# Attention scores on alternating halves of the array, masks added by VectorE, and one projection less in each mixer

## The chip, the cores and the metric

One NeuronCore of a Trainium2 chip runs the whole program. The metric is the device time of one execution in microseconds (us), from the first to the last instruction of the core with what lies around them; lower is better. TensorE multiplies matrices, VectorE (DVE) and ScalarE (ACT) do the elementwise work, and SyncE (SP) starts the transfers.

## The reference, cut to what matters

Two blocks of two layers each on 256 tokens of width 1024. The first block's layer is a feed-forward, a mixer of three kinds of attention, a second feed-forward, and a gated per-layer input. The second block works on the same tokens and on a context of 256 tokens: its layer 0 has a convolution, its layer 1 a windowed attention with sinks over own and context keys.

```python
def masked_softmax(s, mask):
    p = jax.nn.softmax(jnp.where(mask, s.astype(jnp.float32), NEG_BIG), axis=-1)
    return jnp.where(mask, p, 0.0)
# mixer: 4 "nsa" heads (compressed, selected and window keys; one key head of 64 for all),
#        4 "diff" heads (two softmaxes over 32 features each, subtracted), 8 "fox" heads (forget gates):
s = jnp.einsum('bqhd,bkhd->bhqk', qb, k) * scale + (cq[..., :, None] - cT[..., None, :])   # fox
# second block, layer 1: 16 query heads, 4 key heads, |i - j| <= 128, a sink for each head
p = jax.nn.softmax(jnp.concatenate([s_win, s_ctx, sinks], axis=-1), axis=-1)
```

## The kernel before, in words

All is in float32. A matrix of weights comes in tiles of 128 x 1024 (512 KB), and each tile is split into a high part (ACT, a rounded fp32r copy) and a low part (DVE, the rest). A linear layer is then three fp32r products for each 128 x 128 weight block and 256 tokens (`mm3`); this is nearly all of TensorE's work. A product of plain fp32 operands (scores, transposes, values) is one instruction in the code and two MATMUL records in the trace.

**The order is planned.** Streams of work (the main stream, workers for attention heads, the context's stream, the vectors of the adaptive modulation `ada`) are generators that yield before each group of products. `plan()` runs them against `Model`, a simple clock for each engine with prices in ns, and writes down which stream goes on when; the kernel replays that list, so each engine's instructions lie in a fixed order. When no operand of the main work is there, the plan takes a group of a filler stream (context or `ada`).

**The mixer** (one in each of the first block's two layers; about 297 to 470 and 1048 to 1232 us). `project(k)` makes queries and keys with features on partitions, two weight tiles a call, nine calls a layer. `kcmp`, `vcmp`, `kslc` and `kwin` have 64 columns each; their tiles hold these columns twice (`cols_tile(W, l, c, 64, 2)`), so that both halves of the 128 partitions get a copy. `PA` and `PB` hold queries and keys of two heads in a chunk, head i of the pair on partitions 64 i to 64 i + 63. `softmax` (12 calls a layer: 4 for nsa, 4 for diff, 4 for fox) works on such a pair: for head 0 and then head 1 it takes a bank of PSUM, and for the two blocks of 128 queries (against 128 and 256 keys) it issues the score product on that head's 64 partitions (32 for diff; for fox a second product of 16 rows, `LT` and `RT`, adds the gates) and then a bf16 product of the identity with the causal mask (`identb`, `caus`) into the same bank. DVE reduces the maximum, ACT takes the exponential with its sum. `compressed` does the same for 16 compressed keys with 8 small score products, each followed by a mask product. The scaled probabilities are transposed by TensorE and multiplied with the values on 64 of the columns for each head (`values`).

**The second attention** (`attention2`, scores from 2679 us). Three workers take eight chunks c of two heads; `scores(w, c, p, P)` does head p: for each block of queries one product with the own keys (64 rows, 256 columns), one mask product, one product with the context's keys, then the maximum over 512, the sink, and the exponential. PSUM has 8 banks for all streams; the output's projection holds four of them from chunk 0 on.

All products of the scores, masks, values and linear layers are issued at L544, transposes at L561; DVE's `reduce` is L506, `tt` L479, `ts` L486; ACT's `act` is L473. Tiles `m`, `k`, `f`, `fh` are activation buffers, `w` weights, `p` banks of PSUM, `a` raw `ada` and `phi` tiles, `masksb` the masks.

## Time and profile before

| | |
|---|---|
| median of 3 runs | 3006.87 us (3004.06 to 3012.88) |
| profiled execution, span | 3003.3 us |
| TensorE busy | 2944.3 us, 98% |
| VectorE, ScalarE busy | 1957.7 us, 65%; 1409.8 us, 47% |
| mean granted TensorE clock | 0.971 |

The profiled execution is one more execution than the three that are timed; its span, from the first to the last instruction, lies 3.6 us under their median. A matmul's busy time in the profile includes its way through the array, so groups of products overlap one another; what a product costs in a full stream is read from the distance between starts. The clock is given as a share of 2.4 GHz: 0.50 is 1.2 GHz.

### The profile page before, as it was taken

The numbers are of one execution on the slowest core, as the hardware profiler recorded it, in microseconds if no ns is written. First come the engines' busy times: TensorE is split into PE (matmuls) and PEld (weight loads), VectorE is DVE, ScalarE is ACT, GpSimd is POOL, SyncE is SP. The second block draws the span as 40 slices with busy tenths as digits, with TensorE's granted clock in tenths as the row PEclk, the third lists the DMA queues.
The fourth block names the chain that finished last, engine by engine and source line by source line (L and its number), as shares of the span: only waits on it lengthen the run. The fifth ranks groups of instructions, "written<-read, shape, count | busy, mean of one in ns | idle before, by whom it ended". The sixth has DMA issues, their size and how long they took to land.

```text
span 3003.3 us, 56163 instructions
## 1 busy us (share of the span) xinstructions
PE 2944.3 (98%) x23428; PEld 2743.5 (91%) x23428; DVE 1957.7 (65%) x3312; ACT 1409.8 (47%) x2208; POOL 0.2 (0%) x4
## 2 busy tenths in 40 slices
PE   8999999999999999999899999999999999999998
PEld 8989869999999986899789999989999999976898
DVE  5457556656655665588878668888865565566554
ACT  4445334544544543354454554444554454444443
POOL 0000000000000000000000000000000000000000
PEclk9999889999999988899999999999999999999999
DMA  8766524655655554355665556565665565551453
GB/s 291 278 227 212 185 99 134 210 188 174 219 188 190 197 176 143 113 189 184 207 228 181 184 202 200 183 213 183 207 203 185 169 213 193 180 192 35 144 183 119
DMA packets 153278, 555.84 MB, mean 185 GB/s; under 512 B 16320, under 2 KB 26176, under 8 KB 152896
## 3 DMA queue, kind: packets, MB, share of 16 engines
q1 hardware_dynamic: 152304, 550.40, 54.8%
q8 instruction: 184, 3.01, 0.4%
q10 hardware_dynamic: 720, 1.85, 0.2%
q14 instruction: 70, 0.57, 0.1%
HBM read 551.14 MB, written 1.05 MB: 184 GB/s over the span
## 4 chain that ended last, share of the span: by engine, by line
PE 93%; DMA 3%; DVE 2%; ACT 1%; issue 0%; SPq 0%; ACTq 0%; DVEq 0%
PE p L544 92%; DMA a<-ada_w 2%; PE p L561 1%; DMA a<-phi_k 0%; DMA r<-W 0%; DVE m L479 0%; DVE w L479 0%; ACT m L473 0%; DMA a<-phi_v 0%; ACT f L473 0%; DVE m_qn L506 0%; DVE m L494 0%; DMA m_cE<-lam 0%; DVE m L486 0%; SPq L526 0%
## 5 line engine op out<-in xcount | busy, mean ns | idle before, releaser
L544 PE MATMUL p<-m,w 128*128 128x256 f32 x10992 | 1391.1, 284 | 8.0 <-ACT w L473 5.6
L544 PEld LDWEIGHTS p<-m,w 128*128 128x128 f32 x10992 | 1345.8, 191 | 31.9 <-issue 10.3
L479 DVE TENSOR_TENSOR w<-r,w 128x1024 fp32r<-128x1024 f32 (+1 forms) x888 | 1058.6, 1215 | 366.7 <-ACT w L473 365.2
L473 ACT ACTIVATE w<-r 128x1024 fp32r<-128x1024 f32 (+1 forms) x888 | 899.5, 1044 | 370.9 <-PE p L544 280.4
L544 PE MATMUL p<-k,w 128*128 128x256 f32 x4224 | 538.9, 282 | 0.0
L544 PEld LDWEIGHTS p<-k,w 128*128 128x128 f32 x4224 | 515.5, 188 | 9.4 <-issue 5.0
L544 PE MATMUL p<-f,w 128*128 128x256 f32 x3600 | 473.2, 287 | 0.0
L544 PEld LDWEIGHTS p<-f,w 128*128 128x128 f32 x3600 | 449.8, 192 | 9.5 <-issue 5.7
L473 ACT ACTIVATE k<-p 128x256 f32<-128x256 f32 (+1 forms) x200 | 80.7, 404 | 460.9 <-PE p L544 435.6
L479 DVE TENSOR_TENSOR k<-k,p 128x256 f32<-128x256 f32 x176 | 73.9, 420 | 252.8 <-ACT k L473 252.7
L544 PE MATMUL p<-fh,w 128*128 128x256 f32 x1776 | 234.0, 285 | 0.1
L544 PEld LDWEIGHTS p<-fh,w 128*128 128x128 f32 x1776 | 220.7, 191 | 7.5 <-issue 4.9
L479 DVE TENSOR_TENSOR k<-k,k 128x256 fp32r<-128x256 f32 (+1 forms) x176 | 74.9, 425 | 85.5 <-ACT k L473 85.5
L473 ACT ACTIVATE k<-k 128x256 fp32r<-128x256 f32 (+1 forms) x176 | 73.6, 418 | 104.1 <-DVE k L479 104.1
L544 PE MATMUL p<-a,csf 128*32 128x384 f32 x768 | 90.6, 558 | 20.8 <-DMA a<-ada_w 20.8
L494 DVE SCALAR_TENSOR_TENSOR m<-m,vec,m 128x241 f32<-128x241 f32 (+14 forms) x240 | 101.6, 471 | 0.0
L494 DVE SCALAR_TENSOR_TENSOR f<-fh,vec,f 128x241 f32<-128x241 f32 (+14 forms) x240 | 100.8, 471 | 0.0
L473 ACT ACTIVATE m<-m 128x512 f32<-128x512 f32 (+3 forms) x117 | 62.5, 553 | 75.6 <-DVE m L479 35.9
L506 DVE TENSOR_REDUCE m_qn<-p 128x1 f32<-128x128 f32 (+2 forms) x128 | 51.3, 435 | 66.6 <-PE p L544 66.5
L473 ACT ACTIVATE k<-p,m_qn 128x128 f32<-128x128 f32 x96 | 39.4, 417 | 86.2 <-DVE m_qn L506 77.8
L473 ACT ACTIVATE f_sq<-p 128x256 f32<-128x256 f32 x66 | 25.0, 379 | 108.3 <-PE p L544 108.3
L544 PE MATMUL p<-m 64*128 64x128 f32 (+1 forms) x192 | 66.2, 430 | 0.0
(221 smaller groups left out, 1511.8 us busy)
## 6 DMA issues: line engine op xcount, KB each, us to landing
r<-W SPq DMA_DIRECT2D x880, 512.0 KB, 4.3
a<-ada_w SPq DMA_DIRECT2D x96, 768.0 KB, 5.1
a<-phi_k SPq DMA_DIRECT2D x8, 512.0 KB, 6.8
a<-phi_v SPq DMA_DIRECT2D x8, 512.0 KB, 3.5
m<-xT SPq DMA_DIRECT2D x4, 256.0 KB, 4.9
r<-W SPq DMA_DIRECT2D x8, 128.0 KB, 4.7
f<-ctxT ACTq DMA_DIRECT2D x1, 1024.0 KB, 10.7
out<-m SPq DMA_DIRECT2D x4, 256.0 KB, 2.5
```

Source lines behind the costliest of these rows:

```text
L473: self.nc.scalar.activation(out, in_, func, **kw)
L479: self.nc.vector.tensor_tensor(out=out, in0=a, in1=b, op=op)
L494: self.nc.vector.scalar_tensor_tensor(out, a, s, b, op0=op0, op1=op1)
L506: self.nc.vector.tensor_reduce(out, in_, axis=AX, op=op, negate=True)
L544: self.nc.tensor.matmul(out, l, r, start=start, stop=stop, skip_group_check=True)
L561: self.nc.tensor.transpose(out, in_, ident[:k, :k])
```

## The change

- **Scores.** `softmax`, `scores` and the compressed scores take the banks of both heads first and issue one group in which the products of head 0 and head 1 alternate: one on partitions 0 to 63 (or 32 of them), the next on 64 to 127. Fox's product of the gates has 64 rows in place of 16, most of them zero. Before, all of one head's products stood ahead of the other's.
- **Masks.** The mask products on TensorE go (48 in each mixer's pairs, 8 in its compressed scores, and 32 in the second attention). In place of `reduce`, DVE runs `masked`: it adds the mask (bf16, in SBUF) to the scores, turns the sign, writes them back to PSUM and takes the minimum, in one instruction; ACT's exponential then has scale -1. The compressed scores get a `tt` with the mask and then the maximum. `scores` scales both heads' sums at once.
- **Projections.** Eight calls a layer in place of nine: `kcmp` and `vcmp` share a tile, `kslc` and `kwin` share a tile, each column once. `rope_kv` turns the last two with one product and copies them to the other half of the partitions (2 ACT copies of 64 partitions). `compressed` reads its blocks accordingly. The rotation of the nsa queries, the prefix sums and the flags of the fox heads come one `project` earlier.
- **The plan's prices.** A product of 256 fp32r columns is priced 118.2 ns (109.1 before), plain fp32 2.4 ns more, the groups of scores and values with sums of their own, and a group of scores counts 128 rows. The plan of the whole kernel is made anew with these.

```diff
-    masks = np.zeros((128, 288), np.float32)
-    masks[:, :128] = np.where(p[None, :] > p[:, None], NEG, 0.0)
-    masks[:, 128:256] = np.where(p[None, :] < p[:, None], NEG, 0.0)
-    masks[:, 256:] = np.where(okc, 0.0, NEG).reshape(128, 32)
+    masks = np.zeros((128, 672), np.float32)
+    masks[:, :128] = np.where(p[None, :] < p[:, None], NEG, 0.0)
+    masks[:, 512:640] = np.where(p[None, :] > p[:, None], NEG, 0.0)
+    masks[:, 640:] = np.where(okc, 0.0, NEG).reshape(128, 32)
...
-            return max(4 * n / 2.4, 212.0) + 2.4
-        return max(n / 2.4, 94.0 if r.dt == F32R else 53.0) + 2.4
+            return max(4 * n / 2.4, 212.0) + 4.8
+        if r.dt == F32R:
+            return max(0.4508 * n, 106.0) + 2.8
+        return max(n / 2.4, 53.0) + 2.4
...
+    def masked(self, ps, mask, ng):
+        if self.model:
+            self.model.dve(140, 1.04, [ps, ng], [ps, mask])
+        else:
+            self.nc.vector.tensor_tensor_reduce(ps, ps, mask, -1.0, 3e38, OP.add, OP.min, ng)
...
-        rows = 32 * min(g[1].t.shape[1] for g in group)
+        rows = rows or 32 * min(g[1].t.shape[1] for g in group)
         m.pe(cost or sum(m.pe_cost(l, r, r.n) for _, l, r, _, _ in group), rows, reads, writes)
...
-        PC = R.tmp((128, 2, 256), "of", 1)
-        dst = ([PA[:, i:i + 2] for i in (0, 2, 4, 6)] + [PB[:, i:i + 2] for i in (0, 2, 4, 6)] + [PC])
-        keys = [cols_tile(W, l, 256, 64, 2), cols_tile(W, l, 320, 64, 2),
+        PC = R.tmp((128, 256), "of", 1)
+        keys = [cols_tile(W, l, 256), tuple(piece(W, l, kc * 128, kc * 128 + 128, c0, c0 + 64, 0, kc * 128 + q0)
+                                            for kc in range(8) for c0, q0 in ((384, 0), (512, 64))),
                 cols_tile(W, l, 652), cols_tile(W, l, 780), cols_tile(W, l, 908), cols_tile(W, l, 1036),
-                cols_tile(W, l, 0), cols_tile(W, l, 128),
-                cols_tile(W, l, 384, 64, 2), cols_tile(W, l, 512, 64, 2)]
+                cols_tile(W, l, 0), cols_tile(W, l, 128)]
         keys += [cols_tile(W, l, 1420 + 128 * i) for i in (0, 1, 4, 5, 2, 3, 6, 7)]
-        slot = [8, 2, 3, 0, 1, 4, 6, 5, 7]
-        scale = {0: Q_SCALE, 2: D_SCALE, 4: Q_SCALE, 5: Q_SCALE}
+        dst = [None, PA[:, 4:6], PA[:, 6:8], PA[:, 0:2], PB[:, 0:2], PB[:, 4:6], PB[:, 2:4], PB[:, 6:8]]
+        scale = {1: D_SCALE, 3: Q_SCALE, 4: Q_SCALE, 6: Q_SCALE}
...
         def project(k):
             def evac(_, p):
-                d = slot[k]
-                if d in scale:
-                    self.act(dst[d], p, AF.Copy, scale=scale[d])
+                if k == 0:
+                    self.act(PC, p[:, 0])
+                    self.act(PA[:, 2], p[:, 1])
+                elif k in scale:
+                    self.act(dst[k], p, AF.Copy, scale=scale[k])
                 else:
-                    self.cp(dst[d], p)
+                    self.cp(dst[k], p)
             yield from self.lin(R, xs, keys[2 * k:2 * k + 2], evac)
+        def rope_kv():
+            cos, sin = self.rope1[:, 0], self.rope1[:, 1]
+            ps = yield from R.bank((128, 256))
+            raw = PA[:, 2]
+            yield from self.mm(ps, self.con_("perm_n"), raw, True, True)
+            t = R.tmp((128, 2, 256), "sq", 2)[:, 0]
+            self.tt(t, ps, sin, OP.mult)
+            R.banks.put(ps)
+            self.tt(raw, raw, cos, OP.mult)
+            self.tt(PA[64:128, 3], raw[64:128], t[64:128], OP.add)
+            self.tt(PA[0:64, 2], raw[0:64], t[0:64], OP.add)
+            self.act(PA[0:64, 3], PA[64:128, 3])
+            self.act(PA[64:128, 2], PA[0:64, 2])
...
-            for p in range(2):
-                pb = slice(64 * p, 64 * p + 64)
-                ps = yield from R.bank((128, 2, 2, 16))
-                for qb in range(2):
-                    for hh in range(2):
-                        yield from self.mms([(ps[:, qb, hh], PA[pb, hh, qb * 128:qb * 128 + 128], kc[pb], True, False),
-                                             (ps[:, qb, hh], identb, self.maskc[:, qb * 16:qb * 16 + 16], False, True)])
-                self.reduce(NG[:, p], ps, OP.max, negate=True)
+            pss = []
+            for _ in range(2):
+                pss.append((yield from R.bank((128, 2, 2, 16))))
+            yield from self.mms([(pss[p][:, qb, hh], PA[half(p), hh, qb * 128:qb * 128 + 128], kc[half(p)], True, True)
+                                 for qb in range(2) for hh in range(2) for p in range(2)], 1800.0)
+            mc = self.masks[:, 640:672].rearrange("p (q o c) -> p q o c", q=2, o=1).to_broadcast([128, 2, 2, 16])
+            for p, ps in enumerate(pss):
+                self.tt(E[:, p], ps, mc, OP.add)
+                R.banks.put(ps)
+                self.reduce(NG[:, p], E[:, p], OP.max, negate=True)
                 ngb = NG[:, p].rearrange("t q (h o) -> t q h o", o=1).to_broadcast([128, 2, 2, 16])
-                self.tt(E[:, p], ps, ngb, OP.add)
-                R.banks.put(ps)
+                self.tt(E[:, p], E[:, p], ngb, OP.add)
...
-        def softmax(P, sm, ng, qk):
+        def softmax(P, sm, ng, qk, cost=930.0):
+            pss = []
             for i in range(2):
-                ps = yield from R.bank((128, 384))
+                pss.append((yield from R.bank((128, 384))))
+            group = []
+            for qb in range(2):
+                ops = [qk(i, slice(qb * 128, qb * 128 + 128), 128 * (qb + 1)) for i in range(2)]
+                for k in range(len(ops[0])):
+                    group += [(pss[i][:, seg[qb]], *ops[i][k], k == 0, k == len(ops[0]) - 1) for i in range(2)]
+            yield from self.mms(group, cost, 128)
+            for i, ps in enumerate(pss):
                 for qb in range(2):
-                    n = 128 * (qb + 1)
-                    o = ps[:, seg[qb]]
-                    ops = qk(i, slice(qb * 128, qb * 128 + 128), n)
-                    yield from self.mms([(o, a, b, k == 0, False) for k, (a, b) in enumerate(ops)]
-                                        + [(o[:, n - 128:n], identb, self.caus, False, True)])
+                    self.masked(ps[:, seg[qb]], self.masks[:, 512 - 128 * qb:640], ng[:, i, qb:qb + 1])
                 for qb in range(2):
-                    self.reduce(ng[:, i, qb:qb + 1], ps[:, seg[qb]], OP.max, negate=True)
-                for qb in range(2):
-                    self.act(P[:, i, seg[qb]], ps[:, seg[qb]], AF.Exp, bias=ng[:, i, qb:qb + 1],
+                    self.act(P[:, i, seg[qb]], ps[:, seg[qb]], AF.Exp, scale=-1.0, bias=ng[:, i, qb:qb + 1],
                              accum_out=sm[:, i, qb:qb + 1])
...
-                b = slice(64 * i, 64 * i + 16)
-                k = 2 * j + i
+                b, k = half(i), 2 * j + i
                 self.ts(RT[b], cT[b], fm[b, 2 + k:3 + k], fm[b, 10 + k:11 + k], OP.mult, OP.add)
             def qk(i, q, n):
-                b = slice(64 * i, 64 * i + 16)
-                return [(PB[half(i), j, q], PB[half(i), 4 + j, :n]), (LT[b, q], RT[b, :n])]
+                b = half(i)
+                return [(PB[b, j, q], PB[b, 4 + j, :n]), (late[0][b, q], RT[b, :n])]
             P = yield from self.take(R.wk, (128, 2, 384))
-            yield from softmax(P, sm, ng, qk)
+            yield from softmax(P, sm, ng, qk, 1760.0)
...
+        self.spawn(roped(rope_kv(), fl_ + "kv"), 0)
         yield from project(3)
+        def nsa_rope():
+            yield from ropes[1]
+            yield from self.until(fl_ + "kv")
+        self.spawn(roped(nsa_rope(), fl_ + "nsa"), 0)
+        self.spawn(prefix(), 0)
         yield from project(4)
-        self.spawn(roped(ropes[1], fl_ + "nsa"), 0)
-        self.spawn(prefix(), 0)
         yield from project(5)
+        self.flags.add(fl_ + "fox0")
         yield from project(6)
-        self.flags.add(fl_ + "fox0")
         yield from project(7)
-        yield from project(8)
...
-        def scores(w, c, p, P):
+        def scores(w, c, P):
             sm, ng, es = w.small
-            h = head_of(c, p)
-            b = slice(64 * p, 64 * p + 64)
-            sk = self.vec[:, so + h:so + h + 1]
+            sk = [self.vec[:, so + head_of(c, p):so + head_of(c, p) + 1] for p in range(2)]
             for qb in range(2):
-                ps = yield from R.bank((128, 512))
-                ql = q[b, c, qb * 128:qb * 128 + 128]
-                off = 128 * (1 - qb)
-                yield from self.mms([(ps[:, 0:256], ql, k[b, c // 4], True, False),
-                                     (ps[:, off:off + 128], self.identb, (self.caus, self.anti)[qb], False, True)])
-                yield from self.mm(ps[:, 256:512], ql, self.kc2[b, c // 4], True, True)
-                n1 = ng[:, p, qb:qb + 1]
-                self.reduce(n1, ps, OP.max, negate=True)
-                self.stt(n1, sk, -1.0, n1, OP.mult, OP.min)
-                self.act(P[:, qb], ps, AF.Exp, bias=n1, accum_out=sm[:, p, qb:qb + 1])
-                self.act(es[:, p, qb:qb + 1], sk, AF.Exp, bias=n1)
-                R.banks.put(ps)
-            self.tt(sm[:, p], sm[:, p], es[:, p], OP.add)
-            self.recip(sm[:, p], sm[:, p])
-            for qb in range(2):
-                self.ts(P[:, qb], P[:, qb], sm[:, p, qb:qb + 1], None, OP.mult)
+                pss = []
+                for p in range(2):
+                    pss.append((yield from R.bank((128, 512))))
+                at = 256 * (1 - qb)
+                group = []
+                for kk, a in ((k[:, c // 4], at), (self.kc2[:, c // 4], 256 - at)):
+                    for p in range(2):
+                        b = slice(64 * p, 64 * p + 64)
+                        group.append((pss[p][:, a:a + 256], q[b, c, qb * 128:qb * 128 + 128], kk[b], True, True))
+                yield from self.mms(group, 1160.0, 128)
+                for p, ps in enumerate(pss):
+                    n1 = ng[:, p, qb:qb + 1]
+                    self.masked(ps, self.masks[:, 128 * (1 - qb):128 * (1 - qb) + 512], n1)
+                    self.stt(n1, sk[p], -1.0, n1, OP.mult, OP.min)
+                    self.act(P[:, p, qb], ps, AF.Exp, scale=-1.0, bias=n1, accum_out=sm[:, p, qb:qb + 1])
+                    self.act(es[:, p, qb:qb + 1], sk[p], AF.Exp, bias=n1)
+                    R.banks.put(ps)
+            self.tt(sm, sm, es, OP.add)
+            self.recip(sm, sm)
+            for p in range(2):
+                for qb in range(2):
+                    self.ts(P[:, p, qb], P[:, p, qb], sm[:, p, qb:qb + 1], None, OP.mult)
...
-            for p in range(2):
-                yield from scores(w, c, p, P[:, p])
+            yield from scores(w, c, P)
...
-            for kb in range(4):
-                src = (v, self.vc2)[kb // 2]
-                yield from self.mms([(O[64 * p:64 * p + 64], src[:, kb % 2, (2 * (c // 4) + p) * 64:][:, :64],
-                                      T[:, p, kb], kb == 0, kb == 3) for p in range(2)], 480.0)
+            yield from self.mms([(O[64 * p:64 * p + 64], (v, self.vc2)[kb // 2][:, kb % 2, (2 * (c // 4) + p) * 64:][:, :64],
+                                  T[:, p, kb], kb == 0, kb == 3) for kb in range(4) for p in range(2)], 2230.0)
```

## Rows read from the trace of the kernel before

**Rows 1.** The page: busy times, granted clock in 40 slices, the chain's shares by engine.

```profile
PE 2944.3 (98%) x23428; PEld 2743.5 (91%) x23428; DVE 1957.7 (65%) x3312; ACT 1409.8 (47%) x2208; POOL 0.2 (0%) x4
...
PEclk9999889999999988899999999999999999999999
...
PE 93%; DMA 3%; DVE 2%; ACT 1%; issue 0%; SPq 0%; ACTq 0%; DVEq 0%
```

**Rows 2.** Timeline of TensorE, full products: start us, us, line, out<-in, form, records.

```profile
642.38 5.84 PE L544 MATMUL p<-m,w 128*128 128x256 f32 x48
648.06 1.11 PE L544 MATMUL p<-k,w 128*128 128x256 f32 x8
```

**Rows 3.** Timeline of TensorE, one nsa pair's scores in the second mixer.

```profile
1176.11 0.48 PE L544 MATMUL p<-m 64*128 64x128 f32 x2
1176.53 0.23 PE L544 MATMUL p<-masksb,identb 128*128 128x128 bf16 x1
1176.68 0.70 PE L544 MATMUL p<-m 64*128 64x256 f32 x2
1177.31 0.23 PE L544 MATMUL p<-masksb,identb 128*128 128x128 bf16 x1
...
1178.74 0.28 PE L561 MATMUL p<-con,f_row 128*128 128x128 f32 x1
```

**Rows 4.** Timeline of TensorE, one fox head's scores in the second mixer.

```profile
1220.23 0.48 PE L544 MATMUL p<-m 64*128 64x128 f32 x2
...
1222.63 0.48 PE L544 MATMUL p<-m 64*128 64x128 f32 x2
```

**Rows 5.** Timeline of TensorE, one of the eight compressed scores of a layer.

```profile
1122.72 0.39 PE L544 MATMUL p<-m_kc,m 64*128 64x16 f32 x2
1123.04 0.18 PE L544 MATMUL p<-masksb,identb 128*128 128x16 bf16 x1
1123.15 0.39 PE L544 MATMUL p<-m_kc,m 64*128 64x16 f32 x2
```

**Rows 6.** Timeline of TensorE, one head and query block of the second attention.

```profile
2700.09 0.70 PE L544 MATMUL p<-m_of,m 64*128 64x256 f32 x2
...
2701.51 0.85 PE L544 MATMUL p<-a,csf 128*32 128x384 f32 x8
```

**Rows 7.** Timeline of TensorE, two workers' products side by side in the second attention.

```profile
2682.36 0.48 PE L544 MATMUL p<-fh,m 64*128 64x256 f32 x1
2682.36 0.48 PE L544 MATMUL p<-m_of,m 64*128 64x256 f32 x1
...
2682.99 0.23 PE L544 MATMUL p<-masksb,identb 128*128 128x128 bf16 x1
```

**Rows 8.** Busy us by stretch: length, PE, PEld, DVE, ACT, POOL, clock, DMA, GB/s.

```profile
297.00:470.00 173.00, 171.89 (x1120) 132.44 (x1112) 99.06 (x254) 62.41 (x158) 0.00 (x0) 0.88 0.40 135
1048.00:1232.00 184.00, 180.28 (x1127) 134.16 (x1126) 105.56 (x292) 73.36 (x179) 0.00 (x0) 0.83 0.41 141
...
2679.00:2784.00 105.00, 101.35 (x612) 64.42 (x610) 66.13 (x163) 48.63 (x129) 0.00 (x0) 0.97 0.19 63
425.50:442.60 17.10, 17.10 (x54) 10.56 (x54) 5.20 (x19) 4.23 (x17) 0.00 (x0) 0.50 0.00 1
```

**Rows 9.** Timeline of TensorE in the last of these stretches, first and last of 17 lines.

```profile
426.35 0.79 PE L544 MATMUL p<-k,m_LT 16*128 16x128 f32 x2
...
437.93 0.29 PE L544 MATMUL p<-masksb,identb 128*128 128x128 bf16 x1
```

**Rows 10.** The chain that ended last, within 2679 to 2784 us, by line.

```profile
by line: PE p L544 57.9%; PE p L561 11.1%; DVE m_qn L506 5.4%; ACT f L473 5.0%; ACT m L473 3.8%; DVE f L486 3.4%; DVE m L486 2.5%; issue 2.3%; DVE m_qn L494 1.5%; ACT m_nv L473 1.3%; DVE m L479 1.2%; DVE m_qs L514 1.2%; DVE m_qs L479 1.2%; 
```

**Rows 11.** Groups of DVE by form: busy us, mean ns, idle before.

```profile
L479 DVE TENSOR_TENSOR m<-m,p 128x512 f32<-128x512 f32 x53 | 34.9, 681 | 3.3 <-PE p L544 2.5 <-PE p L561 0.8
L506 DVE TENSOR_REDUCE m_qn<-p 128x1 f32<-128x512 f32 x32 | 21.9, 686 | 10.9 <-PE p L544 10.9
```

**Rows 12.** Waits of TensorE: in all us, times, longest.

```profile
PE p L544 <- DMA a<-ada_w: 20.8, 12, 3.8
```

More of the change, by code (lines that the diff above doesn't have):

```diff
@@ L418 @@
 class Soft:
+    pass
 class Stream:
@@ L430 @@
 class Worker:
+    pass
 class Res:
@@ L530, in store, with mms @@
             self.nc.sync.dma_start(dst, src)
-    def mms(self, group, cost=None):
+    def mms(self, group, cost=None, rows=None):
         if self.model:
@@ L537, in mms, with mms_now @@
             yield 0.0
-        self.mms_now(group, cost)
-    def mms_now(self, group, cost=None):
+        self.mms_now(group, cost, rows)
+    def mms_now(self, group, cost=None, rows=None):
         m = self.model
@@ L1200, in mixer, with half @@
             self.tt(ls[:, :, q0:q0 + 8], z, d, OP.add)
-        fm = self.con_("foxm")[:80]
-        cT = R.tmp((80, 256), "cT", 1)
-        LT = R.tmp((80, 256), "LT", 1)
+        fm = self.con_("foxm")
+        cT = R.tmp((128, 256), "cT", 1)
+        late = []
+        def half(i):
+            return slice(64 * i, 64 * i + 64)
         def prefix():
@@ L1224, in compressed @@
                 for par in range(2):
-                    pp = slice(64 * par, 64 * par + 64)
-                    src = PC[pp, a].rearrange("p (c j two) -> p two j c", j=8, two=2)[:, par]
-                    for half in range(2):
-                        pe = self.vec[pp, pe0 + a * 16 + half * 8:pe0 + a * 16 + half * 8 + 8]
-                        self.tt(bf[pp, a, half * 8:half * 8 + 8, :15], src[:, :, half:half + 15],
+                    pa, pp = slice(64 * a, 64 * a + 64), slice(64 * par, 64 * par + 64)
+                    src = PC[pa].rearrange("p (c j two) -> p two j c", j=8, two=2)[:, par]
+                    for hf in range(2):
+                        pe = self.vec[pa, pe0 + par * 16 + hf * 8:pe0 + par * 16 + hf * 8 + 8]
+                        self.tt(bf[pp, a, hf * 8:hf * 8 + 8, :15], src[:, :, hf:hf + 15],
                                 pe.rearrange("p (j o) -> p j o", o=1).to_broadcast([64, 8, 15]), OP.add)
@@ L1351, in values @@
             o = (O[0:64], O[64:128])
-            yield from self.mms([(o[i], V[:, 0, cols(i):cols(i) + 64], T[:, i, 0:256], start, False)
-                                 for i in range(2)], 480.0)
-            yield from self.mms([(o[i][:, 128:256], V[:, 1, cols(i):cols(i) + 64], T[:, i, 256:384], False, stop)
-                                 for i in range(2)], 260.0)
+            yield from self.mms([(o[i], V[:, 0, cols(i):cols(i) + 64], T[:, i, 0:256], start, False) for i in range(2)]
+                                + [(o[i][:, 128:256], V[:, 1, cols(i):cols(i) + 64], T[:, i, 256:384], False, stop)
+                                   for i in range(2)], 860.0)
         def finish(src, c):
@@ L1957, in tables @@
         def tables():
-            mk = self.fr.tmp((128, 288), "sq", 2)
-            self.load(mk, io["masks"], "scalar")
+            for i in range(2):
+                mk = self.fr.tmp((128, 336), "sq", 2)
+                self.load(mk, io["masks"][:, 336 * i:336 * i + 336], "scalar")
+                self.cp(self.masks[:, 336 * i:336 * i + 336], mk)
             self.load(self.rope1, io["rope1"], "scalar")
-            self.cp(mb, mk)
-            self.cp(self.identb, self.con_("ident"))
         self.later = [tables]
```

25 lines of the change are left out of this document (11 added, 14 removed).

## Prediction

> **What bounds the kernel now.** I read the page first: TensorE is busy 98% of the span and makes 93% of the chain that ended last; VectorE and ScalarE have slack on the whole, and the granted clock is below full in two places, the mixers [rows 1]. So work taken from TensorE shortens the span, as long as another stream of the plan fills the place. Then I read prices from the timeline, between starts, since busy times overlap. A full fp32r product of 256 columns costs 5.68 us / 48 = 0.118 us [rows 2]. Third, the stretches: both mixers are full (PE 171.9 of 173 and 180.3 of 184 us), at a mean granted clock of 0.88 and 0.83, with VectorE busy 57% of the time; in the second attention PE is busy 101.4 of 105 us, VectorE 66.1 [rows 8]. There the chain tells more than the busy time: TensorE is 69% of it, the rest mostly the steps of the softmax on VectorE and ScalarE [rows 10].
>
> **Price of a score product.** Alone on its half, one of 128 columns holds TensorE for 0.42 us, one of 256 for 0.63 us [rows 3]. The difference says that 128 columns stream in 0.21 us; the other 0.21 us of each is fixed, and I read it as weights loaded with nothing running over them. What two products on different halves cost, the trace shows once by accident: two workers' products start at the same time and the next one follows 0.63 us later, so two went for the price of one [rows 7]. I take that: a pair of 128 columns for 0.42 us, of 256 for 0.63 us. If the fixed part also vanishes below the other half's stream, the pairs cost 0.21 and 0.43 us; if the halves took turns, 0.84 and 1.26 us. The Trainium skill, "TensorE: Matmul & The Clock Gate", section "What overlaps and what doesn't", says that a weight load runs beside a product in flight only when the row groups differ. By that rule the fixed part would be hidden under alternation; the accidental pair does not show it, and the price stays at 0.63 us.
>
> **The change part by part.**
>
> *Mixer scores.* An nsa or diff pair takes 1178.74 - 1176.11 = 2.63 us, masks included [rows 3]. After: 0.42 + 0.63 = 1.05 us; 1.58 us saved, 16 times (8 a layer): 25.3 us. Diff uses 32 rows a head, but in the same form, and I give it the same price. A fox head takes 1222.63 - 1220.23 = 2.40 us, a pair 4.80 us [rows 4]. After: two pairs of each width, 2.10 us; the 64 rows of the gates' product cost no more than the 16 did: of the 2.40 us two masks take 0.15 us each and the 64-row products 1.05, which leaves the 16-row products the same 1.05 [rows 3, 4]. Saved 2.70 us, 8 times: 21.6 us. A compressed score with its mask takes 0.43 us, without it 0.32 us [rows 5]; eight cost 3.4 us a layer, after between 1.3 us (pairs) and 2.6 us (turns). I take the middle, 1.5 us saved, twice: 3.0 us.
>
> *Projection.* Two weight tiles of 8 blocks with 3 products each fall away a layer: 96 products x 0.118 us = 11.4 us, and with them four loads and four splits, which aren't what TensorE waits for. The rotation loses one fp32 product a layer, at most 0.63 us each; I take 0.9 us in all. `rope_kv` adds short steps on VectorE and ScalarE ahead of the nsa scores. Queued behind them are weight splits; the other projections cover them, since the diff heads go first. If that cover were gone it is some 2 us a layer.
>
> Sum of TensorE's work in the mixers: 25.3 + 21.6 + 3.0 + 11.4 + 0.9 = 62 us. I count it in full, because the fillers' total is fixed: what they do in the mixers needn't be done later.
>
> *Clock.* At half rate a stretch loses what its mean clock lacks: 0.12 x 173 + 0.17 x 184 = 52 us in the two mixers [rows 8]. One such stretch, 425.5 to 442.6 us, is granted 0.50 (1.2 GHz) with VectorE busy only 5.2 of its 17.1 us [rows 8]; from 426.35 to 437.93 us TensorE runs nothing but three fox heads' products on 64 or 16 rows and their masks, one behind the other [rows 9]. So no engine was waited for: what ran there was thin. The change fills both halves in that very work and cuts its length by more than half. But half-rate stretches also follow the compressed branch's small products and stage changes, which stay. I take half back, 25 us; bounds 0 and 52.
>
> *Second attention.* A head and query block takes 1.42 us with its mask [rows 6], both heads 2.84; after, two pairs of 0.63 = 1.26 us. Sixteen times 1.58 us is 25 us of TensorE. It isn't all on the path: 31% of the chain there is softmax steps [rows 10], some products overlap already [rows 7], and 66 us of VectorE stay in a stretch that would shrink to 80. No filler of size is left there. Both heads now also take two banks at once while the output's projection holds four of eight. I take half, 12 us; bounds 0 and 25. The Trainium skill, "TensorEngine Tiling (Array Packing)", section "PSUM Bottleneck", warns that tiling speeds the products and not the emptying of PSUM. By that rule in full, this gain would be zero.
>
> *VectorE's masked step.* 128 of them take the place of 128 reductions. The trace has no such instruction. A maximum over 512 columns takes 0.686 us and a sum of a buffer and a bank of that width 0.681 us [rows 11]; so the new step costs between the same (one pass) and 0.68 us more (two passes). I take it near one pass: 2 us lost on the second attention's chain. In the mixers VectorE has the room: 204.6 of 357 us busy [rows 8].
>
> *New order.* Full products are priced 8% dearer, to what the trace shows, so the plan of the whole kernel changes, the places of the fillers too. The largest wait that an order can move is TensorE's for `ada` tiles, 20.8 us [rows 12]; I give it 0 +- 10 us.
>
> Sum: 62 + 25 + 12 - 2 = 97 us. The profiled span becomes 3003.3 - 97 = 2906 us, and with the 3.6 us by which the span lies under the median, 2910 us.
>
> **The rivals.**
>
> 1. *More comes back.* The weights hide under the other half: 0.41 us more for each of 16 pairs, 0.82 us for each of 8 fox pairs, 0.41 us for 16 groups of the second attention at half: 16 us. The clock gives nine tenths of its 52 us, 46. Then 62 + 16 + 46 + 12 - 2 = 134: 2873 us. For it: the half-rate stretch consists of just this work. Against: the accidental pair showed the fixed part [rows 7]. This is the rule of the page on weights in its full effect.
> 2. *Less.* The clock stays as it is, since stretches of small products remain, and the second attention is held by its softmax chain and the emptying of banks: 62 - 2 = 60: 2947 us. For it: the chain [rows 10], and that removing TensorE's work leaves thinner stretches.
> 3. *Halves take turns* (the change doesn't do what it says). Only the masks and the projection are saved: 0.53 x 16 + 0.60 x 8 + 1.7 + 12.3 + 0.32 x 16 / 2 = 30 us, no clock: 2977 us. The accidental pair speaks against it [rows 7].
> 4. *Slower: VectorE's masked step becomes the bound.* Mixers cut by 87 us leave VectorE 357 - 87 - 204.6 = 65 us free, 0.68 us for each of 96 steps; the second attention 105 - 12 - 66 = 27 us, 0.84 us for each of 32. Beyond some 0.72 us extra, each further us costs 128 us. The whole gain is eaten at 0.72 + 97 / 128 = 1.5 us extra, a step of 2.2 us in place of 0.69. At 2 us extra: 2910 + 1.28 x 128 = 3074 us. For it only that the form is not in the trace; two passes would stay below the point.
>
> **How the numbers follow.** My forecast (2885 to 2935 us) has 0.58, rival 1 0.15, rival 2 0.20, rival 3 0.03, rival 4 0.03; 0.01 for a new order that gives it all back. What a measurement can tell from no change is about 0.3%, 9 us. So faster 0.96, same 0.01, slower 0.03. The range reaches to rivals 1 and 2: 2868 to 2950 us.
>
> **What would show it.** In the changed trace the two heads' score products should start in twos, with some 0.63 us (0.43 to 0.63) for a pair of 256 columns; no `masksb` products on TensorE; 96 fewer `m,w` records. The mixers' stretches should be some 40 us shorter each, with a mean clock above 0.9; a clock as before is rival 2. The second attention should last about 93 us from the first score to the last head, with VectorE's share above 70%. The masked step of 512 columns should take 0.7 to 0.9 us; above 2 us is rival 4. The prediction is wrong if the waits at the stage changes grow by tens of us, for then the new order and not the products decided.

## The result, and the profile after

The changed kernel takes 2952.81 us (median of 4 runs, 2951.42 to 2958.44) beside 3007.56 us for the kernel before: ratio 0.9821 (95% interval 0.9807 to 0.9835), 55 us less. The forecast was 97 us less, and 2950 us the upper end of its range. The profiled execution spans 2949.3 us, at a mean granted clock of 0.976. One run of the kernel with the share 0.15 below took 4459 us at a granted clock of 0.57 and is left out of the median given there.

The page after, the three lines of [rows 1] (busy times, granted clock in 40 slices, the chain by engine):

```profile
PE 2847.2 (97%) x23184; PEld 2689.1 (91%) x23184; DVE 1960.3 (66%) x3423; ACT 1407.1 (48%) x2212; POOL 0.2 (0%) x4
...
PEclk9999999999999999999899989999999999989999
...
PE 87%; DVE 5%; DMA 4%; ACT 3%; issue 1%; SPq 0%; ACTq 0%; DVEq 0%
```

TensorE's busy time fell from 2944.3 to 2847.2 us, by 97.1 us. The span fell by only 54.0. So the time in which TensorE runs nothing rose from 3003.3 - 2944.3 = 59.0 us to 102.1 us. The work that was to go went; 43 us of waiting came, and TensorE's share of the chain fell from 93 to 87%. The 8s of the clock have left the mixers; they stand in slices 20, 24 and 36 now (about 1400, 1700 and 2600 us).

Stretches after (columns as in [rows 8]): the two mixers, the second attention from its first score to its last head's values, and 120 us in the second block's layer 0 that the prediction didn't look at:

```profile
297.00:442.00 145.00, 138.32 (x1154) 115.71 (x1155) 109.78 (x318) 65.48 (x168) 0.00 (x0) 0.98 0.54 185
1018.00:1160.00 142.00, 131.94 (x1071) 100.67 (x1071) 104.13 (x321) 66.22 (x172) 0.00 (x0) 0.94 0.62 213
...
2632.00:2729.30 97.30, 83.13 (x561) 60.43 (x560) 64.61 (x177) 48.21 (x130) 0.00 (x0) 0.89 0.14 44
...
1650.00:1770.00 120.00, 102.50 (x795) 86.40 (x795) 105.34 (x217) 58.54 (x90) 0.00 (x0) 0.87 0.63 217
```

The mixers' clock went from 0.88 and 0.83 to 0.98 and 0.94. The time from a mixer's first score product to its last fell from 155 to 110 us and from 151 to 120 us. But TensorE now idles 7 and 10 us there, 14 in the second attention, and 17.5 in the last stretch.

Prices after. The timeline of TensorE for a fox pair in the second mixer (as [rows 4]; each product of a head is two records, so "x4" is one product for each head), and then the second attention's first scores:

```profile
1141.24 0.49 PE L553 MATMUL p<-m 64*128 64x128 f32 x4
1141.57 0.39 PE L553 MATMUL p<-k,m_ls 64*128 64x128 f32 x4
1141.79 0.60 PE L553 MATMUL p<-m 64*128 64x256 f32 x4
1142.22 0.60 PE L553 MATMUL p<-k,m_ls 64*128 64x256 f32 x4
1142.75 0.38 PE L553 MATMUL p<-f,w 128*128 128x256 f32 x1
...
2632.52 0.60 PE L553 MATMUL p<-fh,m 64*128 64x256 f32 x4
2632.95 0.60 PE L553 MATMUL p<-m_of,m 64*128 64x256 f32 x4
2633.38 0.60 PE L553 MATMUL p<-fh,m 64*128 64x256 f32 x4
```

The fox pair takes 1142.75 - 1141.24 = 1.51 us; it was 4.80 [rows 4] and I expected 2.10. A pair of 256 columns costs 0.43 us inside the group, the bare stream, and 0.53 us as the last of it, ahead of a product on all 128 rows (1142.22 to 1142.75); I took 0.63. Summed from start to next start over the whole trace, waits behind a group's last product included, scores and masks took 143.8 us before and 58.3 after.

VectorE's masked step (form, count, busy, mean ns), beside the plain maximum of [rows 11]; the second line reads its result out:

```profile
L517 DVE CUSTOM_DVE_ANT_0 p<-p,masksb 128x512 f32<-128x512 f32 x32 | 22.2, 695 | 8.8 <-PE p L553 8.8
L517 DVE DVE_READ_ACCUMULATOR2_ANT m_qn<- 128x1 f32 x128 | 18.0, 141 | 0.0
```

Last, where TensorE waits. I summed the trace's gaps without any product and its time at 1.2 GHz by stretches of the span; the last column belongs to an experiment below (12 to 13 us at the two ends of the span come on top):

| stretch of the span | before: gaps, 1.2 GHz | after | share 0.25 |
|---|---|---|---|
| 0 to 1500 us (both mixers) | 17.1, 112 us | 35.5, 44 us | 34.8, 48 us |
| 1500 to 2250 | 11.2, 28 | 21.5, 41 | 5.3, 10 |
| 2250 to the end (second attention) | 17.8, 35 | 32.5, 57 | 27.2, 51 |
| sum | 46.1, 175 | 89.5, 142 | 67.4, 109 |

The clock got better where I expected it and worse elsewhere. What is late there shows in the context's stream. Its convolution has a pointwise layer of 384 `f,w` products, then taps on VectorE, then the keys and values that the second attention needs. That layer's products before a pause and its last ones, the first tap, the end of the keys and values, and the first score, from four places of the timeline after:

```profile
1212.17 0.52 PE L553 MATMUL p<-f,w 128*128 128x256 f32 x3
...
1406.38 1.31 PE L553 MATMUL p<-f,w 128*128 128x256 f32 x9
...
1422.65 0.85 DVE L496 SCALAR_TENSOR_TENSOR f<-fh,vec,f 128x241 f32<-128x241 f32 x2
...
2626.23 5.82 PE L553 MATMUL p<-w,f 128*128 128x256 f32 x48
2631.99 0.70 PE L553 MATMUL p<-m_of,m 64*128 64x256 f32 x4
```

309 of the 384 products are done by 1212 us; the other 75 come at 1395 us, behind the whole second feed-forward of layer 1, beside which the plan gives fillers no share (`FILLS[7]` is 0). So the taps begin at 1423 us; in the kernel before they began at 1300. They end at 1681, 4 us before the main stream's own taps begin (1685). In the stretch 1650 to 1770 VectorE is busy 105 of 120 us, with the one's and then the other's taps, the context has no products to fill with, and what fills is `ada`, for whose transfers TensorE waits 13.9 us there. And the context's last product stands right ahead of the first score at 2632, 100 us after the main stream had begun the norm ahead of that attention; before, it ended at 2519, 160 us ahead of the scores.

### The profile page after: what moved, and what is told of

Its sections match the earlier page's. It is cut to its first block, busy times and chain, and to the rows that moved or that the text cites. A ratio compares the mean times of both kernels' runs of the same rounds, so it can differ in the third digit from the quotient of the medians.

```text
span 2949.3 us, 55792 instructions
## 1 busy us (share of the span) xinstructions
PE 2847.2 (97%) x23184; PEld 2689.1 (91%) x23184; DVE 1960.3 (66%) x3423; ACT 1407.1 (48%) x2212; POOL 0.2 (0%) x4
## 4 chain that ended last, share of the span: by engine, by line
PE 87%; DVE 5%; DMA 4%; ACT 3%; issue 1%; SPq 0%; ACTq 0%; DVEq 0%
PE p L553 86%; DMA a<-ada_w 2%; DVE w L481 1%; PE p L570 1%; ACT k L475 1%; DMA r<-W 1%; DVE m L481 1%; ACT w L475 1%; DVE p L517 1%; ACT m L475 1%; ACT f L475 0%; DMA m_cE<-lam 0%; DVE k L488 0%; DVE m L496 0%; DMA a<-phi_v 0%
## 5 line engine op out<-in xcount | busy, mean ns | idle before, releaser
L553 PE MATMUL p<-k,w 128*128 128x256 f32 x4224 | 553.0, 283 | 0.0
L553 PEld LDWEIGHTS p<-k,w 128*128 128x128 f32 x4224 | 524.7, 188 | 8.8 <-issue 4.4
L553 PE MATMUL p<-f,w 128*128 128x256 f32 x3600 | 489.9, 286 | 0.0
L553 PE MATMUL p<-fh,w 128*128 128x256 f32 x1776 | 243.3, 284 | 0.2 <-ACT k L475 0.2
L475 ACT ACTIVATE m<-m 128x512 f32<-128x512 f32 (+4 forms) x121 | 64.2, 548 | 81.3 <-DVE m L481 39.9
L553 PEld LDWEIGHTS p<-a,csf 128*32 128x32 f32 x768 | 16.9, 115 | 57.0 <-DMA a<-ada_w 40.3
L517 DVE CUSTOM_DVE_ANT_0 p<-p,masksb 128x128 f32<-128x128 f32 (+2 forms) x128 | 56.0, 453 | 14.9 <-PE p L553 13.3
```

The source lines that it names most:

```text
L475: self.nc.scalar.activation(out, in_, func, **kw)
L517: self.nc.vector.tensor_tensor_reduce(ps, ps, mask, -1.0, 3e38, OP.add, OP.min, ng)
L553: self.nc.tensor.matmul(out, l, r, start=start, stop=stop, skip_group_check=True)
```

## The experiments

Two questions: what made a score product cheap, and what took 43 us back.

### What makes a score product cheap

The change does two things at once: it lets halves alternate, and it takes the full-row mask products out from between. Four kernels separate them.

**Issued by head.** Everything as changed, but each group is sorted, so that all products of head 0 stand ahead of head 1's.

```diff
-                    group += [(pss[i][:, seg[qb]], *ops[i][k], ...) for i in range(2)]
+                    group += [(i, pss[i][:, seg[qb]], *ops[i][k], ...) for i in range(2)]
+            group = [g[1:] for g in sorted(group, key=lambda g: g[0])]
```

> The changed kernel with the score products of each group sorted by head: all of head 0's, then all of head 1's, with the same group, banks, masks and planner's price, so the order of everything else is the same. It measures the alternation alone. If alternating runs two products for the price of one or less (0.43 us for a pair of 256 columns against 1.26 by lone prices): TensorE has some 70 us more to do, 50 to 75 us of it seen, 3003 to 3028 us, and half-rate stretches in the mixers come back. If the gain came from the masks and the projection: 2950 to 2975 us.

2952.58 us (0.9824, 0.9801 to 0.9847): the changed kernel's time to 0.3 us, as the second case has it; scores 62.3 us. The order of alternation is worth nothing. The timeline shows why:

```profile
2631.79 0.52 PE L553 MATMUL p<-w,f 128*128 128x256 f32 x3
2632.23 0.71 PE L553 MATMUL p<-m_of,m 64*128 64x256 f32 x4
2632.77 0.60 PE L553 MATMUL p<-fh,m 64*128 64x256 f32 x4
2633.20 0.70 PE L553 MATMUL p<-m_of,m 64*128 64x256 f32 x4
```

There are four records a line of scores still: the two heads' products start 13 ns apart though in the kernel's code one stands behind the other. The halves run side by side without being interleaved there; whether the chip or a step between the code and the chip puts them so, no run shows.

**One head a group.** Masks stay on VectorE; each head has its own bank and its own group, as before.

```diff
-            yield from self.mms(group, cost, 128)
+                    yield from self.mms([(ps[:, seg[qb]], *o, k == 0, ...) for k, o in enumerate(ops)], cost / 4, 128)
```

> Masks stay on VectorE, but no two heads share a group or take two banks at once: every head's score products are issued in a group and a bank of its own, as in the kernel before. If the missing mask products are what made the products cheap, the score products take 58 to 75 us in all (58 in the changed kernel, 144 before) and the time is 2945 to 2970 us. If the two heads' products have to stand side by side in one group, they take 100 us or more, and the time is 2985 to 3010 us.

2957.95 us (0.9842, 0.9824 to 0.9859); scores 71.3 us, both as the first of the two cases has them. The 5 us beside the changed kernel lie within the two intervals. This trace also has one head's products alone, one behind the other on the same half ("x2"):

```profile
2642.61 0.59 PE L553 MATMUL p<-m_of,m 64*128 64x256 f32 x2
2643.04 0.59 PE L553 MATMUL p<-fh,m 64*128 64x256 f32 x2
2643.47 0.59 PE L553 MATMUL p<-m_of,m 64*128 64x256 f32 x2
```

A lone product of 256 columns costs 0.43 us, with no other half to hide its weights. So the 0.63 us of [rows 3] was not the price of a lone product. It is the price between two products on all 128 rows: the first line of a group, with such a product ahead of it, takes 0.54 us (2632.23 to 2632.77 above), the next 0.43, so each side that meets one adds 0.10 us, and 0.43 + 2 x 0.10 = 0.63.

**Masks on TensorE, at the end of each group**, and **behind each head's last product**. The plan's order is the changed kernel's in both; only the place of the mask product in the group differs. VectorE takes the plain maximum. In the first of them a mask is added when another sum has already begun in the same bank, and part of the scores is not the reference's; why was not looked into, and its time is read for the order alone. In the code, `at` is the place of the product behind which a mask goes: the last of the group, or the last of the head and query block.

```diff
+        for k, (out, l, r, start, stop) in enumerate(group):
+            self.nc.tensor.matmul(out, l, r, start=start, stop=False, ...)
+            for at, mo, mask in masks:
+                if at == k:
+                    self.nc.tensor.matmul(mo, self.identb, mask, start=False, stop=True, ...)
```

> The changed kernel with the masks added by products on TensorE again, all of them at the end of each group, behind the last score product; VectorE takes the plain maximum. If a mask product costs only its own stream (some 0.08 to 0.15 us, 128 of them), scores and masks take 68 to 78 us in all and the time is 2955 to 2975 us. If a product on all 128 rows makes its neighbours on 64 rows dear only where the two kinds meet, it is the same, since they meet twice a group. Should masks on TensorE cost as much wherever they stand, scores and masks take over 100 us, and the time is 2990 us or more.

> The same products as with the masks at the end of the group, but each mask product stands right behind the last score product of its head and query block, so full-row products and 64-row products meet several times a group. If meeting is what costs (the 0.21 us of each lone product that did not stream in the kernel before), scores and masks take 100 to 130 us and the time is 2990 to 3020 us. If it is the masks' own stream only, it is the same as with the masks at the end, 2955 to 2975 us.

At the end: 2950.0 us (0.9816, 0.9798 to 0.9834), the changed kernel's time; scores and masks 53.2 + 9.6 = 62.7 us (rounded apart). Both are under the ranges expected. In between: 2997.39 us (0.9972, 0.9962 to 0.9982), 47 us more than that with the same instructions; scores and masks 91.7 + 20.3 = 112 us, as expected. The two timelines, at the end and then in between:

```profile
2632.81 0.70 PE L555 MATMUL p<-m_of,m 64*128 64x256 f32 x4
2633.35 0.60 PE L555 MATMUL p<-fh,m 64*128 64x256 f32 x4
2633.88 0.28 PE L558 MATMUL p<-masksb,identb 128*128 128x128 bf16 x2
2634.10 0.70 PE L555 MATMUL p<-m_of,m 64*128 64x256 f32 x4
```

```profile
2673.19 0.70 PE L555 MATMUL p<-m_of,m 64*128 64x256 f32 x2
2673.82 0.23 PE L558 MATMUL p<-masksb,identb 128*128 128x128 bf16 x1
2673.98 0.70 PE L555 MATMUL p<-m_of,m 64*128 64x256 f32 x2
2674.61 0.23 PE L558 MATMUL p<-masksb,identb 128*128 128x128 bf16 x1
```

In between, "x4" has become "x2": a product on all 128 rows separates the heads, they no longer run side by side, and a lone product is back at 0.63 us with 0.16 for its mask, the prices of the kernel before. Stretches of the first and the second mixer, masks in between:

```profile
297.00:442.00 145.00, 140.44 (x995) 111.33 (x996) 90.01 (x235) 56.29 (x139) 0.00 (x0) 0.89 0.47 165
...
1053.00:1188.00 135.00, 130.80 (x953) 93.46 (x951) 84.55 (x245) 59.76 (x156) 0.00 (x0) 0.95 0.56 195
```

In the first mixer the clock is back at 0.89 as well. In the second it is not: 0.95 from its first score to its last, where the kernel before had 0.82 and the changed one 0.93. So the price of a product, and the first mixer's slow clock, came from the mask products' place; what raised the clock in the second mixer, no run shows. Nor does the place bring all of the price back: scores and masks take 112 us, not 144. Taking the masks off TensorE was one way to move them.

### What took 43 us back

Theories: A, the dearer full product in the plan's prices alone makes the context late; B, the shorter score products do, since they leave fewer holes for the fillers; C, the second attention is held by its own softmax chain, and the context doesn't matter.

**The kernel before with the new prices**, and **the changed kernel with the old prices.**

```diff
-            return max(4 * n / 2.4, 212.0) + 2.4
-        return max(n / 2.4, 94.0 if r.dt == F32R else 53.0) + 2.4
+            return max(4 * n / 2.4, 212.0) + 4.8
+        if r.dt == F32R:
+            return max(0.4508 * n, 106.0) + 2.8
+        return max(n / 2.4, 53.0) + 2.4
```

> The kernel before with one edit: the planner prices a product of 256 fp32r columns at 118.2 ns in place of 109.1 and plain fp32 2.4 ns more, as the change does. The work is the same; the order is planned anew. Theory A (the dearer price alone lets the context's stream fall behind, its keys come after the second attention has begun, and that costs the time that is missing): slower than before by 30 to 60 us, 3037 to 3067 us, the context's last products within 30 us of the first scores of the second attention. Theory B (the context falls behind because the shorter score products leave fewer gaps to fill): no change, 2997 to 3017 us.

> The changed kernel with one edit undone: full products and plain fp32 are priced as before (109.1 ns for 256 fp32r columns). Theory A: the context is early again and the time falls to 2890 to 2915 us, what the prediction's sum gives without the lag. Theory B: the lag stays, 2945 to 2960 us. Theory C (the second attention is held by its own softmax chain and by taking two banks at once, not by the context): 2945 to 2960 us too, with the stretch from the first to the last score still some 92 us and the waits around it as they were.

The prices alone: 3044.98 us (1.0129, 1.0110 to 1.0148), 37 us slower with the same products. The context's last products start at 2712.56, the first score at 2718.30 us. The changed kernel with the old prices: 2971.58 us (0.9884, 0.9865 to 0.9903), between what A and B expected. There, too, the last 9 products of the pointwise layer stay behind until 1404 us, and the context ends at 2648, right ahead of the first score. So each edit by itself is enough to make the context late, and the two don't add. The same prices that cost the kernel before 37 us are worth 19 us in the changed one (2952.81 beside 2971.58).

**Share of the second mixer 0.25.** The changed kernel with one number other: fillers may take 0.25 of the main stream's time beside the second mixer.

```diff
-FILLS = (0.25, 0.1, 0.05, 0, 0, 0.05, 0.08, 0, 0.5, ...
+FILLS = (0.25, 0.1, 0.05, 0, 0, 0.05, 0.25, 0, 0.5, ...
```

> The changed kernel with one number changed: the share of TensorE's time that the plan lends to filler streams in the second mixer goes from 0.08 to 0.25. No work is added or taken. If the late context is what costs the time (A or B): its last products come before the second attention's queries, the stage from its normalization to the next one shrinks from 206 us to about 165, and the time falls by 20 to 45 us to 2908 to 2933 us. Theory C: no change, 2945 to 2960 us, with the stage still near 200 us.

2916.80 us (0.9703, 0.9684 to 0.9721), 36 us less than the changed kernel. First tap, end of the context and first score in its timeline, and then the stretch 1650 to 1770 us:

```profile
1221.35 0.47 DVE L496 SCALAR_TENSOR_TENSOR f<-fh,vec,f 128x241 f32<-128x241 f32 x1
...
2526.94 5.46 PE L553 MATMUL p<-w,f 128*128 128x256 f32 x45
...
2592.01 0.70 PE L553 MATMUL p<-m_of,m 64*128 64x256 f32 x4
```

```profile
1650.00:1770.00 120.00, 120.00 (x1019) 118.85 (x1018) 82.26 (x127) 62.57 (x89) 0.00 (x0) 1.00 0.57 198
```

The taps begin 201 us earlier, the context is ready 60 us ahead of the scores, and the stretch that idled 17.5 us is full at full clock: 343 of the context's `f,w` products lie there, nearly all ahead of the main stream's taps (from 1754 us). By the table, gaps and clock between 1500 and 2250 us make up 16 + 31 / 2 = 32 of the 36 us. The main stream shows them later: it reaches the norm ahead of the second attention 14 us after the changed kernel does, but from that norm to the next it takes 158 us in place of 206, as expected, and the context is done before it begins. C falls as the account of these 36 us; the attention's own stretch stays as long as it was, 99 us from the first score to the last head beside 97.

**Share of the second feed-forward 0.15.** The mixers as changed; only the 0 that held the last 75 products is lifted.

```diff
-FILLS = (..., 0.08, 0, 0.5, ...
+FILLS = (..., 0.08, 0.15, 0.5, ...
```

> The changed kernel with one number other: the share that fillers get beside the second feed-forward of layer 1, 0 in both kernels, is 0.15; the mixers' shares are as in the changed kernel. If the context is late because the last fifth of its pointwise layer is held over that whole stage (309 of 384 products were done by 1212 us, the other 75 at 1395 to 1407 us, and its taps on VectorE began at 1423 us), those 75 come before 1300 us, the context is ready before the second attention's first scores are asked for, and the time is 2910 to 2935 us. If the share of the mixer mattered for another reason, the time stays at 2945 us or more.

2927.03 us (median of three runs; 0.9748, 0.9719 to 0.9776), as expected. The 75 products come by 1279 us, the first tap at 1282, the context ends at 2548 and the scores begin at 2604. So it was the held rest of that layer.

**Controls: the kernel before with the larger share**, and **with the new prices and a larger share in the first mixer** (0.4 for 0.05).

> Control: the kernel before, with nothing changed but the share that fillers get beside the second mixer, 0.25 in place of 0.08. In the kernel before the context's pointwise layer is complete inside that mixer and the context is ready before the second attention asks for it, so if the share only cures the lag there is nothing to cure: 2995 to 3020 us. If the larger share is worth something by itself, with or without the change, the kernel before gains as the changed one did, some 35 us: 2960 to 2985 us.

> Control for the prices: the kernel before with the new prices of full products, which alone took 3045 us, and the share of the first mixer 0.4 in place of 0.05, so that the context starts early. If the new prices cost their 37 us only by the lag of the context, the time comes back to 2995 to 3020 us. If the order under the new prices is worse for another reason, it stays above 3030 us.

The first: 3023.81 us (1.0045, 1.0029 to 1.0061), a little slower. The share is worth nothing where the context is in time. It has little to move there: the pointwise layer ends at 1289 us in place of 1294, so it was not complete inside the mixer's scores (to 1225 us) in the kernel before either, only without a pause behind them. With the share 0.25 on both sides, the change is worth 1.0045 - 0.9703 = 3.4%, some 103 us. The second: 3030.14 us (1.0067, 1.0042 to 1.0091), above the 2995 to 3020 of the lag alone and right at the 3030 of its rival. By the ratios about half of what the prices cost came back (1.29% to 0.67%). The rest is open: this share also lengthened the first mixer's scores from 156 to 189 us, and no run separates the two.

**Other shares on the changed kernel.**

```diff
+FILLS = (0.25, 0.1, 0.05, 0, 0, 0, 0.1, 0.05, 0.5, 0.25, 0.08, 0.08, ...      # a
+FILLS = (0.25, 0.1, 0.25, 0, 0, 0.05, 0.08, 0, 0.25, 0.25, 0.08, 0.6, ...     # b
```

> The changed kernel with three shares other: beside the first feed-forward of layer 1 0 in place of 0.05, beside its mixer 0.1 in place of 0.08, beside its second feed-forward 0.05 in place of 0. If a little filler work beside the second feed-forward is enough to end the pointwise layer, and holding less in the mixer keeps the main stream ahead, the context is in time and the time is 2900 to 2925 us. If the lag needs the larger share in the mixer, 2935 us or more.

> The changed kernel with shares other that bring the context earlier still: beside the first mixer 0.25 in place of 0.05, second mixer as it is, second feed-forward of layer 1 0 as it is; later shares 0.25 in place of 0.5 and 0.6 in place of 0.08. The pointwise layer should be complete inside the second mixer, the context ready before the second attention: 2900 to 2930 us. If filler work beside the first mixer costs there what it saves later, 2935 us or more.

2921.00 us (0.9703, 0.9689 to 0.9718) and 2918.57 us (0.9695, 0.9675 to 0.9715). Three ways of getting the context ready early end within 5 us of one another, all below the changed kernel by 32 to 36 us; the fourth, the share beside the second feed-forward, by 26. Other shares were not run.

The lag is not all of the 43 us. With the share 0.25 the gaps of the table fall from 89.5 to 67.4 us, 22 of the 43; the other 21 stay: 18 more than before up to 1500 us, 9 more behind 2250, and 6 fewer between. What TensorE lacks in these gaps was not tested.

## Why the prediction was right or wrong

**The sum of TensorE's work was nearly right.** Scores and masks lost 143.8 - 58.3 = 85.4 us (from unrounded sums), of which I had 75 (25.3 + 21.6 + 3.0, and 25 in the second attention); the projection's 96 products, 11.4 us, are gone as worked out; together 97 us, the fall of the busy time. The clock's part lies within these sums, since many of the old score products ran at 1.2 GHz. That the forecast's sum is 97 us too is chance: it has 25 us of clock in it and 12 of the 25 us of the second attention.

**The price of a pair was taken too high**, 0.63 instead of 0.43 us. The failing step is the reading "the other 0.21 us of each is fixed, and I read it as weights loaded with nothing running over them". [rows 3] was true, but it showed a product between two mask products; the run with masks in between brings the 0.21 us back with alternating halves. This error made the forecast's gain too small, so it is not what put the time off; the next two steps are. The Trainium skill, "TensorE: Matmul & The Clock Gate", section "What overlaps and what doesn't", says that a weight load runs beside a product in flight only when the row groups differ. This case's traces don't agree: in the kernel with one head a group, products on the same half follow one another in 0.43 us, the bare stream. The accidental pair [rows 7] stood between two products on all rows too, its mask and this one right ahead of it:

```profile
2681.83 0.59 PE L544 MATMUL p<-m,con 128*128 128x256 f32 x2
```

**"I count it in full, because the fillers' total is fixed" failed.** The total is fixed, but its place isn't free: the context's products can only go where their inputs are ready, and the second attention waits for the last of them. In the changed kernel the context's taps came 122 us later, and both streams' taps then stood one behind the other on VectorE, while TensorE had nothing of the context to fill with. That cost 36 us, the difference between the changed kernel and the one with the share 0.25.

**"I give it 0 +- 10 us", of the new order, failed.** The new prices alone made the kernel before 37 us slower, and in the changed kernel they are worth 19 us the other way; one share of the fillers, which changes nothing but the order, is worth 36. I took the largest wait that I saw, for `ada` tiles [rows 12]; it did rise by only 10 us:

```profile
PE p L553 <- DMA a<-ada_w: 30.4, 19, 3.8
```

But an order moves more than waits that are there already. In the profile of before I had no wait for the context at all, because it was 160 us early; I didn't ask how early, nor what it depended on. The text's last line named this case ("if the waits at the stage changes grow by tens of us"), and only 0.01 was kept, for an order that gives all of the gain back: rival 2 gives nearly this time, 2947 us, but by a clock that stays, and the mixers' clock did not stay.

**Clock: the size was too small in the mixers, and the mechanism is shown for the first of them alone.** By the two stretches, 0.02 x 145 + 0.06 x 142 = 11 us are lost there now; it was 52, so 41 came back, and not 25. The run with masks in between, where products stand one behind the other again, has the low clock again in the first mixer (0.89), not in the second (0.95). And behind 1500 us the time at 1.2 GHz rose from 63 to 98 us (the table), another 17 us lost. Without the lag (share 0.25) it is 61 us, as before.

**Second attention:** 97 us from the first score to the last head, predicted 93, so 7 us were gained of the 12; TensorE idles 14 us of it and runs at 0.89. VectorE's share is 64.6 of 97.3, 66%, not above 70%. By what the Trainium skill says in "TensorEngine Tiling (Array Packing)", section "PSUM Bottleneck", taken in full, nothing would have been gained there; the stretch went from 104 us [rows 8] to 97. It is 97 us with the masks at the end of each group too, and 103 with them in between. The scores start in twos. **Masked step:** 0.695 us, near the one pass that I took, with a readout of 0.141 us behind it that I hadn't counted: 18.0 us of VectorE over the whole kernel, where it has slack. Rival 3 (halves take turns) and rival 4 (the masked step) are excluded by these rows.

With the context in time, the changed kernel takes 2917 to 2927 us by the four ways, near the forecast of 2910. That is partly luck: the pair and the mixers' clock brought more than I counted, and gaps in the mixers (35 us before 1500 us in place of 17, in the kernel with the share 0.25 too) took it back.

## What to carry to other kernels

Before counting freed time on the bounding engine in full, ask of each stream that fills it when its result is needed, how early it is now, and which step of it waits for a whole layer; a stream that shows no wait may be just in time. When a plan is remade, let it be remade alone (new prices, old kernel) and see what that costs. In these kernels products on half of the rows ran side by side and at full stream, interleaved in the code or not, as long as no product on all rows stood between them. Where one does, see first whether it can go to the end of the group: that was worth 47 us here with the same instructions, though the sums in the banks would have to be laid out so that they stay right, which no run here has.

## What the runs showed of the hardware

- Products on different halves of the rows start 7 to 13 ns apart at the head of a group, also when the kernel's code has all of one half's ahead of the other's (the changed kernel, and issued by head).
- A 64-row product of 256 columns takes 0.43 us in a stream of its own kind, 0.63 between products on 128 rows and 0.53 to 0.54 with one such product beside it: some 0.10 us for each meeting. A 128 x 128 bf16 mask product takes 0.16 us between 64-row products; two of them one behind the other take 0.22 us together (2633.88 to 2634.10).
- One masked add and minimum over 512 columns, written back to PSUM, takes 0.695 us, and reading out its result another 0.141.
